# Second layer's output projection by seven quarter products

## The chip, the cores and the metric

The kernel runs on one core of one Trainium2 chip. A core has a matrix engine (PE, with its weight loads shown apart as PEld), VectorE (DVE), ScalarE (ACT), GpSimd (POOL), a queue engine that issues transfers (SP) and 16 DMA engines. The metric is device time in microseconds for one execution, the median of several runs. The profile is one execution taken by the hardware profiler.

## The reference

Two encoder layers over 512 tokens of width 1024. Layer 0 mixes tokens by neighbourhood attention (16 heads of 64, a window of 8 x 16 on a 64-wide grid), layer 1 by multi-head latent attention (16 heads). All is fp32.

```python
for i in range(DEPTH):                       # DEPTH = 2
    xn = rmsnorm(x, norm_g[i])
    y = mixer_na(...) if i % 2 == 0 else mixer_mla(...)
    h = x + y
    gate = jax.nn.sigmoid(rmsnorm(h, ple_norm[i]) @ ple_w_gate[i])   # 512x1024 @ 1024x1024
    x = h + gate * (p[i] @ ple_w_proj[i])
return rmsnorm(x, final_norm)
```

Both mixers end in `(o * silu(z)) @ w_out`: the heads' rows `o`, multiplied element by element by a gate branch, times a 1024x1024 matrix. That last product of layer 1 is what the change is about.

## The kernel before

**Precision.** Every fp32 matrix product is made of three passes in the format float32r: an operand is split into a rounded part `hi` (a copy on ACT) and a rest `lo` (a subtraction on POOL or DVE), and hi x hi, lo x hi and hi x lo are added up in PSUM. So a product of two 128x128 by 128x512 blocks is three matmuls, and every weight that comes from memory costs a copy of 128x1024 on ACT and a subtraction of the same size before PE can use it. `load_w` (L79 to L90) does that for one piece: a raw buffer (three in all), `whi`, `wlo` (three of each, in a pool shared by the whole kernel), or buffers `w4` of the stage's own pool.

**Stages.** Layer 0: the gate branch, the heads (`na_heads`), the output projection (`out_proj`), the embedding's gate (`gate_seven`). Layer 1: compressions (`mla_c`), the heads (`mla_heads`), `out_proj`, `gate_seven`, final norm.

**The latent attention** (`mla_heads`) is a loop of 70 steps. Step i takes scores of one query tile of one head (`score`: maximum on DVE L844, exponential on ACT L846, normalisation on POOL L848), transposes those of step i - 3 on PE (`turn`, L139), and every few steps multiplies by the values (`output`, L863). Projections of later heads and the product of the per-layer embedding (`ple`) are cut in pieces and laid among them. Two heads make one tile of rows; `gated` (L207 to L213) multiplies it by the gate branch `z` on POOL and splits it to `oT`, tile j of which holds rows 128 j to 128 j + 127 of `o` transposed.

**The output projection** (`out_proj`, L411 to L428) goes by halves n of the output's 1024 columns and by the four token tiles t. Each of the eight results is 24 matmuls of 128x512 into a bank of PSUM; DVE adds it to the residual row (L427), and `turn_h` (L1043) then scales the row on DVE (L1047), transposes it on PE and hands it to `keep_half` (L538), which makes the gate's operands from it. The residual rows `r` are loaded from memory at the start of the stage (L1035).

**The gate** (`gate_seven`, L568) already multiplies by Strassen's scheme in Winograd's form: tokens, inner dimension and output columns are each cut in two, and the eight quarter products become seven, with sums of quarters on both sides. The sums of the weights' quarters are made by DMA in memory: `sum_step` issues, on POOL's queue, a copy or an accumulating transfer of 1 MB; eight of these make a layer's four sums. The heads of layer 0 issue them for both layers, one per head (16). The sums of the activations are made in `keep_half` and `mixed`.

**Order.** On each engine instructions run in the order of the program that the build's planner settles, with its own estimates of durations. `tc.issue_after(x)` puts what follows behind x on that engine's queue. Buffers of a pool are taken from those that are free.

## Time and profile before

| what | value |
|---|---|
| time, median of 3 runs | 657.52 us (657.03 to 657.75) |
| span of the profiled execution | 655.8 us; the page gives no other time of it |
| PE busy | 646.2 us (99% of the span) |
| DVE, ACT, POOL busy | 398.1, 441.2, 433.8 us (61, 67, 66%) |
| DMA | 102.18 MB, mean 156 GB/s |
| heads of layer 1 | to about 565 us |
| output projection of layer 1 on PE | about 554 to 608 us, first matmuls among the last heads' |
| gate of layer 1 on PE | about 608 to 647 us |

PE's busy time counts matmuls whose ends are modelled, so that 99% says that PE always had a matmul under way, not that it ran at its peak. Rows of a view by stretch give the stretch, its length, then busy time and count for each engine, the granted clock of PE (1.00 is full), the share of DMA time and the rate. Rows of a view in order of time give start and length, both in us; "x3" is three of them, one behind the other; in square brackets stands the idle time before and what ended it. Rows of groups give busy time and the mean in ns of one.

### The profile page before, as it was taken

The numbers are of one execution on the slowest core, as the hardware profiler recorded it, in microseconds if no ns is written. First come the engines' busy times: TensorE is split into PE (matmuls) and PEld (weight loads), VectorE is DVE, ScalarE is ACT, GpSimd is POOL, SyncE is SP. The second block draws the span as 40 slices with busy tenths as digits, with TensorE's granted clock in tenths as the row PEclk, the third lists the DMA queues.
The fourth block names the chain that finished last, engine by engine and source line by source line (L and its number), as shares of the span: only waits on it lengthen the run. The fifth ranks groups of instructions, "written<-read, shape, count | busy, mean of one in ns | idle before, by whom it ended". The sixth has DMA issues, their size and how long they took to land.

```text
span 655.8 us, 10132 instructions
## 1 busy us (share of the span) xinstructions
PE 646.2 (99%) x3419; PEld 551.6 (84%) x3419; DVE 398.1 (61%) x854; ACT 441.2 (67%) x879; POOL 433.8 (66%) x383
## 2 busy tenths in 40 slices
PE   9999999999999999999999999999999999999994
PEld 6888888998988888888899888888888888888884
DVE  6190355845646526569825613888888886464665
ACT  7672587766767743687743635897979897537855
POOL 0496475895685664697764626785969887436974
PEclk9999999999999999999999999999999999999998
DMA  9944254996675889435743334120111223673524
GB/s 329 348 134 140 96 197 134 249 233 143 215 161 184 199 171 373 169 129 157 252 120 114 103 98 148 51 76 5 64 55 65 65 71 123 226 287 129 191 67 160
DMA packets 44756, 102.18 MB, mean 156 GB/s; under 512 B 4640, under 2 KB 17696, under 8 KB 44704
## 3 DMA queue, kind: packets, MB, share of 16 engines
q1 hardware_dynamic: 33776, 83.97, 38.1%
q0 software_dynamic: 10496, 16.78, 11.8%
q10 hardware_dynamic: 432, 0.79, 0.3%
q8 instruction: 27, 0.44, 0.3%
q14 instruction: 25, 0.20, 0.1%
HBM read 89.99 MB, written 25.17 MB: 176 GB/s over the span
## 4 chain that ended last, share of the span: by engine, by line
PE 98%; ACT 0%; DVE 0%; issue 0%; POOLq 0%; POOL 0%
PE ps_mm L107 35%; PE ps_S L107 12%; PE ps_mm L751 7%; PE ps_T L139 6%; PE ps_T L643 5%; PE ps_O L863 5%; PE ps_mm L643 3%; PE ps_S L643 3%; PE ps_T L107 3%; PE ps_T L238 2%; PE ps_O L400 2%; PE ps_O L107 2%; PE ps_mm L701 2%; PE ps_mm L184 2%; PE ps_T L388 2%; PE ps_S L701 1%
## 5 line engine op out<-in xcount | busy, mean ns | idle before, releaser
L84 POOL TENSOR_TENSOR wwlo<-wraw,wwhi 128x1024 fp32r<-128x1024 f32 (+5 forms) x78 | 143.2, 1852 | 76.4 <-ACT wwhi L83 54.7
L83 ACT ACTIVATE wwhi<-wraw 128x1024 fp32r<-128x1024 f32 (+5 forms) x81 | 65.5, 832 | 61.1 <-issue 19.2
L588 POOL TENSOR_TENSOR wlo<-wraw,whi 128x512 fp32r<-128x512 f32 x56 | 73.6, 1346 | 25.2 <-ACT whi L586 19.0
L848 POOL TENSOR_TENSOR ex<-ex,rc 128x512 f32<-128x512 f32 x64 | 66.3, 1045 | 25.8 <-DVE rc L847 22.0
L846 ACT ACTIVATE ex<-ps_S,mx 128x512 f32<-128x512 f32 x64 | 44.0, 688 | 11.7 <-DVE mx L844 10.1
L844 DVE TENSOR_REDUCE mx<-ps_S 128x1 f32<-128x512 f32 x64 | 43.7, 682 | 8.3 <-PE ps_S L107 7.7
L96 DVE TENSOR_TENSOR pt_lo<-ps_T,pt_hi 128x512 fp32r<-128x512 f32 x64 | 43.1, 681 | 7.1 <-ACT pt_hi L94 6.7
L374 POOL TENSOR_TENSOR ex<-ex,rc 128x128 f32<-128x128 f32 (+1 forms) x64 | 36.1, 621 | 15.0 <-DVE rc L370 15.0
L107 PE MATMUL ps_mm<-xh,wwhi 128*128 128x512 f32 x152 | 40.3, 398 | 0.0
L94 ACT ACTIVATE pt_hi<-ps_T 128x512 fp32r<-128x512 f32 x64 | 37.8, 595 | 3.4 <-PE ps_T L139 3.0
L107 PE MATMUL ps_mm<-xl,wwhi 128*128 128x512 f32 x152 | 38.5, 391 | 0.0
L139 PE MATMUL ps_T<-ident,ex 128*128 128x128 f32 x256 | 38.3, 272 | 0.0
L107 PE MATMUL ps_mm<-xh,wwlo 128*128 128x512 f32 x152 | 38.2, 391 | 0.0
L139 PEld LDWEIGHTS ps_T<-ident,ex 128*128 128x128 f32 x256 | 31.5, 140 | 7.5
L107 PEld LDWEIGHTS ps_mm<-xh,wwlo 128*128 128x128 f32 x152 | 28.3, 188 | 6.0
L586 ACT ACTIVATE whi<-wraw 128x1024 fp32r<-128x1024 f32 x28 | 29.2, 1055 | 5.9 <-DMA wraw<-sum 3.0
L107 PEld LDWEIGHTS ps_mm<-xl,wwhi 128*128 128x128 f32 x152 | 28.3, 188 | 5.7
L205 DVE TENSOR_TENSOR u<-ps_O,u 64x512 f32<-64x512 f32 x32 | 22.0, 686 | 17.2 <-ACT u L204 16.7
L368 ACT ACTIVATE ex<-ex,mx 128x128 f32<-128x128 f32 (+1 forms) x64 | 30.3, 475 | 2.7 <-DVE mx L358 1.8
L107 PEld LDWEIGHTS ps_mm<-xh,wwhi 128*128 128x128 f32 x152 | 27.3, 188 | 4.8
L209 POOL TENSOR_TENSOR u<-u,z 128x512 f32<-128x512 f32 x16 | 21.9, 1371 | 13.6 <-DVE u L205 8.3
L107 PE MATMUL ps_S<-ko,qo 128*128 128x512 f32 x96 | 28.9, 409 | 0.0
(441 smaller groups left out, 1849.8 us busy)
## 6 DMA issues: line engine op xcount, KB each, us to landing
sum<-gate POOLq DMA_DIRECT2D x12, 1024.0 KB, 7.8
wraw<-na_qk SPq DMA_DIRECT2D x16, 512.0 KB, 3.4
wraw<-sum SPq DMA_DIRECT2D x16, 512.0 KB, 3.3
pe<-pe SPq DMA_DIRECT2D x31, 256.0 KB, 6.9
wraw<-gate SPq DMA_DIRECT2D x12, 512.0 KB, 3.3
wraw<-na_v SPq DMA_DIRECT2D x8, 512.0 KB, 4.1
sum<-sum POOLq DMA_DIRECT2D x4, 1024.0 KB, 10.9
wraw<-na_o SPq DMA_DIRECT2D x8, 512.0 KB, 5.4
```

The lines of the kernel that those rows point to most:

```text
L83: nc.scalar.activation(hi[:, c], raw[:, c], AF.Copy)
L84: f = lambda e, c=c: e.tensor_tensor(out=lo[:, c], in0=raw[:, c], in1=hi[:, c].bitcast(F32), op=ALU.subtract)
L94: self.last_copy = nc.scalar.activation(hi, src, AF.Copy, scale=scale)
L96: nc.vector.tensor_tensor(out=lo, in0=src, in1=hi.bitcast(F32), op=ALU.subtract)
L107: last = self.last_mm = nc.tensor.matmul(out, l, r, start=i == 0, stop=i == n - 1)
L139: self.last_mm = self.nc.tensor.transpose(t[:, i * P:(i + 1) * P], b, self.ident)
L588: nc.gpsimd.tensor_tensor(out=lo[:, o], in0=raw[:, o], in1=hi[:, o].bitcast(F32), op=ALU.subtract)
L643: mm = nc.tensor.matmul(ps, l, r, start=j == 0 and p in banks, stop=j == 11 and p in (2, 3, 4), skip_group_check=True)
L751: self.last_mm = nc.tensor.matmul(PS[key], *terms[i], start=i == 0, stop=i == len(terms) - 1)
L844: nc.vector.reduce_max(mx, sp, axis=AX.X, negate=True)
L846: nc.scalar.activation(ex, sp, AF.Exp, bias=mx, accum_out=sm)
L848: nc.gpsimd.tensor_tensor(out=ex, in0=ex, in1=rc.to_broadcast([P, S]), op=ALU.mult)
```

## The change

The output projection of layer 1 is made by the same scheme of seven products (`out_seven`); layer 0 keeps `out_proj`. `MIXED` names the layers for which this holds.

- **Weights.** `sum_step` gets a key in place of a layer, and there is a third set of sums, for the matrix of the output projection. Layer 0's heads issue the sums of both gates, now those of layer 1 first. The eight transfers for the projection are issued in `score` of layer 1, one per head, behind the normalisation of the second query tile of heads 1 to 8.
- **Rows.** `gated_seven` takes the place of `gated` in layer 1. It writes the gated product over `z`, and mixes halves of tokens with DVE: for the first four tiles the difference goes to `oT` in place of the second half; for the other four, `zs` of tile j and of tile j - 4 are mixed in place.
- **Products.** `out_seven` loads 14 weight pieces (`piece_of`) in place of 8, splits the mixed rows to `Y` and `Y3`, and runs 7 x 2 x 12 matmuls, chained in one order. Products 2, 4, 5 and 3 go on in the bank in which 1, 7 and 6 ended, which DVE reads in between. What DVE reads is added to or taken from the residual rows, up to three rows per half product.
- **The gate's operands** come in another order of rows, so that `keep_mixed` makes them, the operand of product 3 among them (before: `mixed(3)`, in the gate).
- **Order of loads.** The residual rows are loaded behind the first four weight pieces. `gn`, and the gate's loads of the embedding, follow the last weight load of the projection, which is now its fourteenth.

```diff
+MIXED = (1,)
+LO, HI = slice(0, 256), slice(256, 512)
...
+        for key in [("gate", l) for l in SEVEN] + [("out", l) for l in MIXED]:
+            self.sums[key] = {p: dram.tile([2 * P, D], F32, name=f"sum{key[0]}{key[1]}{p}") for p in (4, 5, 6, 7)}
...
-            attend(j, lambda e: self.sum_step(l, 2 * step + e))
+            key = (("out", 0) if 0 in MIXED else ("gate", 1), ("gate", 0))[j // 4]
+            attend(j, lambda e: self.sum_step(key, 2 * (j % 4) + e))
...
+    def piece_of(self, pool, key, p, c, after=None, rest=None):
...
+        own = self.pieces % (3 + self.wxn // 2) < 3
+        self.pieces += 1
+        src = self.quarter[key][p] if p < 4 else self.sums[key][p]
+        raw = self.wp.tile([P, 1024], F32, name="wraw", tag="wraw", bufs=3)
+        q, n = (self.wp, 3) if own else (pool, self.wxn)
+        hi, lo = (q.tile([P, 1024], F32R, name=t, tag=t if own else "w4", bufs=n) for t in ("whi", "wlo"))
+        self.last_load = nc.sync.dma_start(raw, src[c * P:(c + 1) * P])
+        with self.tc.issue_after(after.ins) if after else nullcontext():
+            nc.scalar.activation(hi, raw, AF.Copy)
+        for o in (slice(0, S), slice(S, 2 * S)):
+            (rest or nc.gpsimd).tensor_tensor(out=lo[:, o], in0=raw[:, o], in1=hi[:, o].bitcast(F32), op=ALU.subtract)
...
+    def gated_seven(self, u, zs, oT, j):
...
+        nc.gpsimd.tensor_tensor(out=z, in0=u, in1=z, op=ALU.mult)
+        sub = lambda o, x, y: nc.vector.tensor_tensor(out=o, in0=x, in1=y, op=ALU.subtract)
...
+        if g == 0:
+            sub(u[:, HI], z[:, LO], z[:, HI])
+            for x, c in ((z, LO), (u, HI)):
+                nc.scalar.activation(hi[:, c], x[:, c], AF.Copy)
+                nc.gpsimd.tensor_tensor(out=lo[:, c], in0=x[:, c], in1=hi[:, c].bitcast(F32), op=ALU.subtract)
+            return
+        nc.scalar.activation(hi, z, AF.Copy)
+        nc.gpsimd.tensor_tensor(out=lo, in0=z, in1=hi.bitcast(F32), op=ALU.subtract)
+        y = zs[k]
+        sub(y[:, HI], y[:, HI], z[:, HI])
+        sub(y[:, LO], y[:, LO], y[:, HI])
+        sub(z[:, LO], z[:, LO], y[:, LO])
...
+    def out_seven(self, pool, layer, oT, zs, res, after, last_mm):
...
+        order = (1, 7, 2, 4, 6, 5, 3)
+        prep = lambda p: W.__setitem__(p, [self.piece_of(pool, key, p, c, rest=nc.vector if c and p in (1, 7, 2) else None)
+                                           for c in range(2)])
+        for p in order[:2]:
+            prep(p)
+        for t in range(NT):
+            nc.sync.dma_start(res[t], self.a["x"][t] if layer == 0 else self.spill[t])
+        for p in order[2:4]:
+            prep(p)
...
+        for k in range(4):
+            nc.scalar.activation(Y[0][:, k, :], zs[k], AF.Copy)
+            nc.vector.tensor_tensor(out=Y[1][:, k, :], in0=zs[k], in1=Y[0][:, k, :].bitcast(F32), op=ALU.subtract)
+        for k in range(4):
+            nc.scalar.activation(y3[0][:, k, :], zs[4 + k][:, LO], AF.Copy)
+            nc.vector.tensor_tensor(out=y3[1][:, k, :], in0=zs[4 + k][:, LO], in1=y3[0][:, k, :].bitcast(F32),
+                                    op=ALU.subtract)
+        src = {1: ([x[0] for x in oT], 0), 7: ([x[0] for x in oT], 256), 2: ([x[1] for x in oT], 0),
+               4: ([x[1] for x in oT], 256), 6: (Y, 0), 5: (Y, 256), 3: (y3, 0)}
+        banks = {1: "mm", 7: "S", 6: "T"}
+        home = {2: 1, 4: 7, 5: 6, 3: 6}
...
+        for n, p in enumerate(order):
+            if 0 < n < 4:
+                prep(order[n + 3])
...
+            for i in range(2):
...
+                for j, (l, r) in enumerate(m):
+                    with self.tc.issue_after(mm):
+                        self.last_out = nc.tensor.matmul(ps, l, r, start=j == 0 and p in banks,
+                                                         stop=j == 11 and p in (2, 4, 3), skip_group_check=True)
+                    mm = self.last_out.ins
+                for t, h, op in {1: ((0, 1, 0), (2, 1, 0), (2, 0, 1)), 7: ((2, 1, 0),), 2: ((0, 0, 1),), 4: ((2, 0, 1),),
+                                 6: ((2, 0, 0),), 5: ((2, 1, 1),), 3: ((0, 1, 1),)}[p]:
+                    r = res[t + i][:, h * S:(h + 1) * S]
...
+                if p in (2, 6, 5, 3):
+                    after(t + i, h)
...
+    def keep_mixed(self, t, n, ps):
...
+        if (t < 2, n) == (True, 0):
+            self.operand(1, i, ps)
+            keep = self.AC[i] = self.temp("a")
+            nc.scalar.activation(keep, ps, AF.Copy)
+        elif n == 0:
+            c = self.C[i] = self.temp("c")
+            nc.scalar.activation(c, ps, AF.Copy)
+            nc.vector.tensor_tensor(out=ps, in0=self.AC[i], in1=ps, op=ALU.subtract)
+            self.operand(7, i, ps)
+            nc.scalar.activation(self.AC[i], ps, AF.Copy)
+        elif t >= 2:
+            self.operand(4, i, ps)
+            nc.vector.tensor_tensor(out=self.C[i], in0=self.C[i], in1=ps, op=ALU.subtract)
+            nc.vector.tensor_tensor(out=ps, in0=self.AC[i], in1=ps, op=ALU.add)
+            self.operand(6, i, ps)
+            nc.scalar.activation(self.AC[i], ps, AF.Copy)
+        else:
+            self.last_pair = self.operand(2, i, ps)
+            nc.vector.tensor_tensor(out=ps, in0=ps, in1=self.AC[i], op=ALU.subtract)
+            self.operand(3, i, ps)
...
+            norm = nc.gpsimd.tensor_tensor(out=ex, in0=ex, in1=rc.to_broadcast([P, S]), op=ALU.mult)
+            step = h - 1
+            if qt == 1 and 0 <= step < 8 * len(later):
+                with self.tc.issue_after(norm.ins):
+                    self.sum_step(later[step // 8], step % 8)
...
-                    ps = self.transposes([hg[:, i * P:(i + 1) * P] for i in range(4)])
+                    ps = self.transposes([hg[:, i * P:(i + 1) * P] for i in range(4)],
+                                         "O" if layer in MIXED and t % 2 else "T")
...
+                if layer in MIXED:
+                    self.out_seven(pool, layer, oT, zs, res, turn_h, last)
```

107 lines of the change are left out of this document (61 added, 46 removed).

## Prediction

> **What bounds the kernel now.** I read the page first: the engines' busy time and the shares of the chain of waits.
>
> ```profile
> span 655.8 us, 10132 instructions
> PE 646.2 (99%) x3419; PEld 551.6 (84%) x3419; DVE 398.1 (61%) x854; ACT 441.2 (67%) x879; POOL 433.8 (66%) x383
> PE 98%; ACT 0%; DVE 0%; issue 0%; POOLq 0%; POOL 0%
> ```
>
> PE is the chain for 98% of the span. A matmul taken off PE is a saving, unless PE then waits. So I looked at the other engines around the place of the change, with busy time by stretch (columns: stretch, length, PE, PEld, DVE, ACT, POOL, granted clock, DMA share, GB/s).
>
> ```profile
> 400.00:492.00 92.00, 92.00 (x508) 77.90 (x508) 75.99 (x152) 77.13 (x170) 68.42 (x66) 1.00 0.20 58
> 464.00:480.00 16.00, 16.00 (x98) 13.84 (x97) 14.31 (x30) 14.41 (x33) 15.68 (x16) 1.00 0.29 79
> 554.00:570.00 16.00, 16.00 (x78) 13.25 (x77) 5.45 (x8) 8.51 (x14) 6.89 (x5) 1.00 0.44 150
> 570.00:586.00 16.00, 16.00 (x77) 13.32 (x77) 12.16 (x11) 4.77 (x6) 5.34 (x3) 1.00 0.94 360
> 586.00:608.00 22.00, 22.00 (x108) 18.30 (x107) 10.52 (x18) 16.45 (x27) 15.45 (x14) 1.00 0.36 121
> 608.00:641.00 33.00, 33.00 (x160) 27.82 (x159) 23.78 (x38) 22.19 (x38) 28.18 (x23) 1.00 0.39 128
> ```
>
> PE has no gap anywhere, at full clock. The attention of the second layer (first two rows) leaves POOL 15.68 of 16 us busy in its densest stretch. The output projection (554 to 608) has spare POOL and ACT time, but 0.94 of the DMA at 570 to 586. The gate behind it keeps POOL at 28.18 of 33 us.
>
> **Removed: 24 matmuls.** The projection has 2 x 4 x 24 = 192 matmuls of 128x512; seven products of 2 x 12 are 168. The chain of waits prices a steady stream of that shape in the gate, which already works by seven products.
>
> ```profile
> 625.08 16.32 PE ps_T L643 x72
> ```
>
> 16.32 / 72 = 0.2267 us, times 24 = **5.44 us saved**. The 32 transposes of `turn_h` stay, so PE gains no work. The bounds are 0 and 5.44: all the rest of the change can only make PE wait.
>
> **Added in the attention: eight accumulating DMAs on POOL.** The first layer's heads issue 16 such DMAs before and after, in another order. The eight new ones go one per head, behind the normalisation of its second query tile. Six read a quarter, two read a sum.
>
> ```profile
> L522 POOL DMA_DIRECT2D sum<-gate x12: 771/922/1347, 89.3 to 234.5; - x12
> L522 POOL DMA_DIRECT2D sum<-sum x4: 1274/1294/1313, 125.2 to 224.6; - x4
> sum<-sum POOLq DMA_DIRECT2D x4, 1024.0 KB, 10.9
> ```
>
> That is 6 x 0.922 + 2 x 1.294 = 8.1 us of POOL's time within the first stretch above, where POOL idles 92.00 - 68.42 = 23.6 us. Behind each issue wait the next normalisation, its transposes on PE, and what follows them. The last sum lands some 11 us after its issue, over 50 us ahead of the projection, so landing costs nothing. How late may a normalisation be? Here POOL's row of two of them, and PE's transposes of the first:
>
> ```profile
> 466.76 2.03 POOL L848 TENSOR_TENSOR ex<-ex,rc 128x512 f32<-128x512 f32 x2
> 468.46 0.60 PE L139 MATMUL ps_T<-ident,ex 128*128 128x128 f32 x4
> ```
>
> The first is done at 466.76 + 1.015 = 467.78, 0.68 us ahead of its transposes, in the densest of the stretches. One issue of 0.92 in the queue before it makes PE wait 0.25 us or so; the eight issues meet two or three such places. I take **+0.6 us**; the bounds are 0 and 8.1 (every issue on PE's path).
>
> **Added: the mixing of gated rows.** `gated_seven` adds DVE subtractions of 128x256: one for each of the first four head pairs, three for each of the others, 16 in all. By the 0.43 us row below, 6.9 us, of which DVE has 92.00 - 75.99 = 16.0 us free in the first 92 us alone. The splits of `Y` and `Y3` (four of 512 and four of 256 on ACT and on DVE) are needed by the fifth product, 96 matmuls or 21.8 us after the first begins, and at 0.69 us and less a piece they take some 4.5 us of each engine. Taken at 0, bounds 0 and 1.
>
> ```profile
> L649 DVE TENSOR_TENSOR ps_S<-ps_S,s 128x256 f32<-128x256 f32 x1 | 0.4, 424 | 0.0
> ```
>
> **Moved: which weights the first matmuls need.** This is where I expect the gain to leak. Before, all tokens start on the first weight piece; after, a product consumes two pieces in 5.44 us, and the matmuls are chained in one order. The end of attention, by the chain of waits and by the rows of the weight splits:
>
> ```profile
> 561.10 0.69 DVE L96 TENSOR_TENSOR pt_lo<-ps_T,pt_hi 128x512 fp32r<-128x512 f32 x1 [0.37 <-ACT pt_hi L94]
> 554.73 1.39 PE ps_S L107 x6
> 561.13 1.15 PE ps_S L107 x5
> 562.28 1.37 PE ps_mm L107 x6
> 563.65 1.81 PE ps_O L863 x8
> 544.96 1.06 ACT L83 ACTIVATE wwhi<-wraw 128x1024 fp32r<-128x1024 f32 x1 [0.50 <-PE ps_mm L751]
> 562.05 1.23 DVE L84 TENSOR_TENSOR wwlo<-wraw,wwhi 128x1024 fp32r<-128x1024 f32 x1 [0.26 <-ACT wwhi L83]
> 563.53 2.39 POOL L84 TENSOR_TENSOR wwlo<-wraw,wwhi 128x1024 fp32r<-128x1024 f32 x1 [7.40 <-ACT wwhi L83]
> 568.75 2.94 ACT L83 ACTIVATE ww<-wraw 128x1024 fp32r<-128x1024 f32 x3
> 569.83 1.47 DVE L84 TENSOR_TENSOR ww<-wraw,ww 128x1024 fp32r<-128x1024 f32 x1 [3.01 <-ACT ww L83]
> 570.83 2.73 POOL L84 TENSOR_TENSOR ww<-wraw,ww 128x1024 fp32r<-128x1024 f32 x1 [0.60 <-ACT ww L83]
> 578.82 2.39 POOL L84 TENSOR_TENSOR ww<-wraw,ww 128x1024 fp32r<-128x1024 f32 x1 [5.26 <-ACT ww L83]
> L1035 SPq DMA_DIRECT2D r<-spill x4: 383/423/443, 566.4 to 567.8; - x4
> DMA to landing us min/median/max: 2.8/4.1/6.7
> ```
>
> Before, some 17 projection matmuls stand among the last heads' work up to 563.65, all on the first piece. After, that piece serves six (first half of product 1, tokens 0 to 127); the next six need the second piece, whose buffers the per-layer embedding holds until 561 and whose rest is done at 562.05 + 1.23 = 563.3. So 11 matmuls (2.5 us) lose their place as cover. The last output products can move up to fill most of it, since their last operand is there at 561.10 + 0.69 = 561.8: I leave 0.7 us open. From 563.3 PE has 18 matmuls of product 1 and six of product 7 (third piece, ready at 565.9) = 5.4 us, to 568.7. The fourth piece, on the `w4` buffers, came at 569.83 + 1.47 = 571.3; the heads' last rows are let go one split earlier now (`u` is read only by the product with `z`), so about 570: 1.0 us more. Product 2 accumulates into the bank of product 1, and waits until DVE has read it three times per half, for all four residual rows. The last of these landed at 567.8 + 6.7 = 574.5, about when product 7 ends (570 + 18 x 0.2267 = 574.1): 0.2 us. Product 4 wants its pieces at 580; they follow the raw buffers, behind the residual rows, to about 580 and 582.5. The norm and embedding loads, tied behind the last weight load, now leave that stretch and help. Together **+1.9 us**; the bounds are 0 (all overlap) and 5.4 (three full halves and the bank wait in a row).
>
> **Added: work behind each product.** DVE adds 18 products' reads to rows in place of 8; more than that, the products 6, 5 and 3 share one pair of banks, so that each half waits until DVE has read the half before it, with 12 matmuls = 2.72 us of other work in between. By rows of 0.69 (one read), 0.75 (`hg`) and 0.69 (operands), DVE has 2.8, 4.2 and 3.5 us behind each half of these three: 21.0 in all, against 3 x 5.44 + 24 x 0.109 (a transpose) = 18.9 of PE.
>
> ```profile
> L427 DVE TENSOR_TENSOR r<-ps_mm,r 128x512 f32<-128x512 f32 x4 | 2.8, 692 | 4.5 <-PE ps_mm L107 4.5
> 583.13 0.75 DVE L1047 SCALAR_TENSOR_TENSOR hg<-r,rowb,gp 128x512 f32<-128x512 f32 x1
> 604.04 0.87 PE ps_T L139 x8
> ```
>
> The 2.1 us of lag fall mostly on the gate's first two products (10.9 us of cover, their operands come from products 2 and 6). I take **+0.4**, bounds 0 and 2.1. Without the cover it is 2.1.
>
> **Added: six more pieces to split.** ACT is busy 51.9 of the 87 us from 554 to 641 (the last four stretches), and six pieces at 1.05 add 6.3. POOL gets 11 projection pieces (three of 14 go to DVE) where it had four. Its rate, in the gate, below the last rows that the heads leave it, and PE's last matmul:
>
> ```profile
> 568.93 1.29 POOL L213 TENSOR_TENSOR o1l<-u,o1h 128x512 fp32r<-128x512 f32 x1 [0.74 <-ACT o1h L212]
> 604.30 10.50 POOL L588 TENSOR_TENSOR wlo<-wraw,whi 128x512 fp32r<-128x512 f32 x8
> 615.28 7.56 POOL L588 TENSOR_TENSOR wlo<-wraw,whi 128x512 fp32r<-128x512 f32 x6
> 624.13 3.33 POOL L588 TENSOR_TENSOR wlo<-wraw,whi 128x512 fp32r<-128x512 f32 x2 [1.28 <-issue]
> 646.59 0.40 PE L643 MATMUL ps_O<-wlo,X 128*128 128x256 f32 x2
> ```
>
> 10.50 / 4 = 2.63 us a piece, against 2.72 us that PE takes to use one: POOL just keeps up, so 0, with the case that it doesn't as a rival.
>
> **The sum.** 655.8 - 5.44 + 0.6 + 1.9 + 0.4 = 653.3 for the profiled span. The median of the runs, 657.52, is 1.7 above that span (the page gives no other time of that execution), so **655.0 us**.
>
> **Rivals.** *Full gain*: the planner, which settles each engine's order, closes all holes: 657.52 - 5.44 = 652.1. For it: PE has no gap before, with all these waits around. Against: the first pieces' times. *Gain used up*: the start costs 5 in place of 1.9, or several terms come near their upper ends: 657.4. For it: a product wants two pieces every 5.44 us from a standing start, on a DMA at 0.94. *POOL becomes the bound* (slower): from 568.9, where the last heads' rows are on POOL, 23 pieces remain to it until the end, with four small powers and one product (3.5 us), and 18 matmuls (4.1 us) run after the last piece. The last matmul of before ends at 646.9, so the point from which it decides is (646.9 - 568.9 - 3.5 - 4.1) / 23 = 3.06 us a piece. Two rows stand below it (2.63, 2.52), one above (3.33). At 3.2 the end moves by 23 x 0.14 = 3.2 us: 660.7. What could lift it is DVE work beside it:
>
> ```profile
> 579.26 3.17 DVE L1047 SCALAR_TENSOR_TENSOR hg<-r,rowb,gp 128x512 f32<-128x512 f32 x2
> 571.73 2.92 DVE L84 TENSOR_TENSOR ww<-wraw,ww 128x1024 fp32r<-128x1024 f32 x1 [0.42 <-ACT ww L83]
> ```
>
> Both ran while POOL split weights; alone the two would have taken 1.5 and 1.22. The Trainium skill, "SBUF — State Buffer", section "SBUF: two separate sides", says that DVE operations with two SBUF inputs and GpSimd operations take a shared port pair in turn, and the loser waits for the whole instruction. These two rows agree. By that rule each of the added `Y` rests would stand between two of POOL's, an estimate of 4 x 0.69 + 4 x 0.43 = 4.5 us over 23 pieces, or 2.83 a piece: near the point, not over it; the sum stays at 655.0 by the rule and by the rows, and the rule is why this rival has more than a token chance. *The DMA issues push the attention* (slower): all 8.1 us on PE's path, with the other terms, 655.0 - 0.6 + 8.1 = 662.5; half of it, 658.5. Against: 23.6 us of idle POOL.
>
> **Chances.** Forecast 0.40, its own range 653.0 to 656.2; full gain 0.20; gain used up 0.18; POOL the bound 0.15; attention pushed 0.07. A measurement can tell 0.2% (1.3 us): faster 0.60, same 0.18, slower 0.22. The range is 651.8 to 659.6: below lies nothing that PE's count allows but the spread of runs, above about the half of the two slow cases.
>
> **What would show it.** 168 matmuls of 128x512 in place of 192. PE gaps between 554 and 583, ended by weight splits or by DVE's reads: 1 to 3 us in all; none says full gain, over 4 says used up. Gaps before L139's transposes between 418 and 490: under 1 us. In the gate, PE waiting for POOL's rests would show the POOL rival; a piece then takes over 3 us. I am wrong as well if the last matmul ends under 2 us or over 5 us earlier than 646.9.

## The result, and the profile after

The changed kernel takes **681.31 us** (median; 679.05 to 683.75), against 657.49 for the kernel before beside it: ratio 1.0364, 95% interval 1.0340 to 1.0389. The forecast was 655.0, its range ended at 659.6. The first lines of the page, and the shares of the chain of waits:

```profile
span 677.3 us, 10188 instructions
...
PE 649.9 (96%) x3395; PEld 551.6 (81%) x3395; DVE 424.4 (63%) x890; ACT 451.8 (67%) x897; POOL 465.3 (69%) x413
...
PE 79%; DVE 7%; ACT 5%; POOL 4%; DMA 3%; issue 2%; POOLq 0%; SPq 0%; DVEq 0%; ACTq 0%
```

The 24 matmuls are gone (3419 to 3395), but PE's busy time rose by 3.7 us, and PE is the chain for 79% of the span in place of 98%. The same stretches as before, and two more (columns as before: stretch, length, PE, PEld, DVE, ACT, POOL, granted clock, DMA share, GB/s):

```profile
400.00:492.00 92.00, 88.25 (x468) 74.13 (x467) 77.11 (x142) 71.67 (x159) 73.08 (x74) 0.96 0.51 131
464.00:480.00 16.00, 12.25 (x48) 9.47 (x48) 13.92 (x22) 8.88 (x21) 11.21 (x12) 0.79 0.47 128
469.00:478.00 9.00, 7.71 (x26) 6.06 (x27) 7.24 (x16) 5.91 (x15) 6.10 (x6) 0.62 0.31 118
...
570.00:586.00 16.00, 12.97 (x48) 9.55 (x46) 13.25 (x19) 6.58 (x12) 9.09 (x6) 0.89 0.86 311
586.00:608.00 22.00, 20.12 (x93) 16.41 (x94) 12.76 (x19) 11.18 (x14) 20.04 (x15) 1.00 0.66 212
608.00:641.00 33.00, 24.30 (x120) 20.46 (x119) 22.25 (x34) 26.77 (x41) 30.81 (x26) 0.85 0.58 189
```

At 464 to 480 PE did 48 matmuls where it did 98, with POOL busy for 11.21 us and not fuller than before (15.68). And the clock, 1.00 in every stretch before, is 0.62 to 0.89 where PE had stood still. PE's own rows show the stops (in square brackets the idle time and what ended it):

```profile
468.98 0.63 PE L147 MATMUL ps_T<-ident,ex 128*128 128x128 f32 x4 [2.46 <-POOL o1l L554]
470.90 1.65 PE L115 MATMUL ps_S<-ke,qe 96*128 96x512 f32 x3 [1.29 <-ACT ex L951]
...
578.13 0.73 PE L605 MATMUL ps_S<-whi,o1h 128*128 128x512 f32 x2 [1.48 <-ACT whi L537]
586.27 0.70 PE L605 MATMUL ps_mm<-whi,o1h 128*128 128x512 f32 x2 [1.72 <-DVE r L612]
602.70 0.66 PE L147 MATMUL ps_T<-ident,hg 128*128 128x128 f32 x4 [1.61 <-DVE hg L1158]
...
631.07 1.12 PE L147 MATMUL ps_O<-ident,hg 128*128 128x128 f32 x4 [2.57 <-ACT a L675]
638.31 1.19 PE L748 MATMUL ps_O<-whi,X 128*128 128x256 f32 x4 [6.13 <-DVE X L628]
```

These seven are 17.3 us; smaller ones make it 18.0. The ledger: the span grew by 677.3 - 655.8 = 21.5 us although 5.44 were saved, so the change cost 26.9. Of that 18.0 are gaps of PE; the other **8.9 us, the remainder, are matmuls that ran slower behind the gaps**. By stage the gaps are 4.4 us in the attention, 4.8 in the projection and 8.7 in the gate; from the spacing of the same matmuls before and after I count another 3.6, 2.7 and 2.4 us for the clock.

### The profile page after: what moved, and what is told of

The parts are those of the page before. It is cut to its first block, busy times and chain, and to the rows that moved or that the text cites. A ratio compares the mean times of both kernels' runs of the same rounds, so it can differ in the third digit from the quotient of the medians.

```text
span 677.3 us, 10188 instructions
## 1 busy us (share of the span) xinstructions
PE 649.9 (96%) x3395; PEld 551.6 (81%) x3395; DVE 424.4 (63%) x890; ACT 451.8 (67%) x897; POOL 465.3 (69%) x413
## 3 DMA queue, kind: packets, MB, share of 16 engines
q0 software_dynamic: 15744, 25.17, 17.3%
## 4 chain that ended last, share of the span: by engine, by line
PE 79%; DVE 7%; ACT 5%; POOL 4%; DMA 3%; issue 2%; POOLq 0%; SPq 0%; DVEq 0%; ACTq 0%
PE ps_mm L115 30%; PE ps_S L115 8%; PE ps_T L748 5%; PE ps_mm L856 4%; PE ps_T L147 4%; PE ps_mm L748 2%; PE ps_T L246 2%; PE ps_O L972 2%; PE ps_O L407 2%; PE ps_S L748 2%; PE ps_mm L806 2%; PE ps_T L115 2%; PE ps_mm L192 2%; PE ps_T L395 2%; POOL wlo L539 1%
## 5 line engine op out<-in xcount | busy, mean ns | idle before, releaser
L92 POOL TENSOR_TENSOR wwlo<-wraw,wwhi 128x1024 fp32r<-128x1024 f32 (+5 forms) x76 | 139.1, 1852 | 67.0 <-ACT wwhi L91 45.4
L539 POOL TENSOR_TENSOR wlo<-wraw,whi 128x512 fp32r<-128x512 f32 x78 | 105.2, 1380 | 30.3 <-ACT whi L537 25.6
L91 ACT ACTIVATE wwhi<-wraw 128x1024 fp32r<-128x1024 f32 (+5 forms) x78 | 62.5, 824 | 60.1 <-issue 19.1
L953 POOL TENSOR_TENSOR ex<-ex,rc 128x512 f32<-128x512 f32 x64 | 68.8, 1095 | 24.3 <-DVE rc L952 17.5
L537 ACT ACTIVATE whi<-wraw 128x1024 fp32r<-128x1024 f32 x42 | 44.1, 1057 | 20.2 <-DMA wraw<-sumout 7.8
L115 PE MATMUL ps_S<-ke,qe 96*128 96x512 f32 x96 | 29.4, 415 | 1.3 <-ACT ex L951 1.3
```

The lines of the kernel that those rows point to most:

```text
L91: nc.scalar.activation(hi[:, c], raw[:, c], AF.Copy)
L92: f = lambda e, c=c: e.tensor_tensor(out=lo[:, c], in0=raw[:, c], in1=hi[:, c].bitcast(F32), op=ALU.subtract)
L115: last = self.last_mm = nc.tensor.matmul(out, l, r, start=i == 0, stop=i == n - 1)
L537: nc.scalar.activation(hi, raw, AF.Copy)
L539: (rest or nc.gpsimd).tensor_tensor(out=lo[:, o], in0=raw[:, o], in1=hi[:, o].bitcast(F32), op=ALU.subtract)
L953: norm = nc.gpsimd.tensor_tensor(out=ex, in0=ex, in1=rc.to_broadcast([P, S]), op=ALU.mult)
```

## The experiments: the gate and its one bank

**Reading.** The kernel's PSUM banks go by the names mm, S, T and O; there are 2, 2, 3 and 1 of them. Before, transposes of finished rows went to the three T banks. Now those of odd rows go to bank O, of which there is one, and which the gate also uses for the last half of its product 7 (a half of 256 columns). These are the rows of ACT and DVE around the gap at 638, with POOL's weight rests beside them:

```profile
630.42 0.60 ACT L675 ACTIVATE a<-ps_O 128x512 f32<-128x512 f32 x1 [0.27 <-DVE X L628]
...
632.36 0.58 ACT L627 ACTIVATE X<-ps_O 128x512 fp32r<-128x512 f32 x1
```

```profile
632.97 0.69 DVE L628 TENSOR_TENSOR X<-ps_O,X 128x512 fp32r<-128x512 f32 x1 [2.25 <-ACT X L627]
633.58 0.69 DVE L678 TENSOR_TENSOR ps_O<-ps_O,a 128x512 f32<-128x512 f32 x1
634.18 3.39 DVE L628 TENSOR_TENSOR X<-c,X 128x512 fp32r<-128x512 f32 x2
637.49 0.68 DVE L628 TENSOR_TENSOR X<-ps_O,X 128x512 fp32r<-128x512 f32 x1
```

```profile
625.42 20.75 POOL L539 TENSOR_TENSOR wlo<-wraw,whi 128x512 fp32r<-128x512 f32 x16
```

Row 3 holds the bank until ACT's copy `a` at 630.4 (first gap, 2.57 us), then row 1's second half goes in and is read five times, the last read behind two operands of product 5 (`X<-c,X`) that take 1.7 us each. Only then may product 7 start its last half: 6.13 us. Two runs take the bank away from one or the other user.

*a_bankT*: one of the four odd transposes to T.

```diff
-                                         "O" if layer in MIXED and t % 2 else "T")
+                                         "O" if layer in MIXED and t % 2 and (t, n) != (1, 1) else "T")
```

> The changed kernel with one bank moved: the last transposes of the projection (row 1, second half) go to a bank of the three T in place of the single O, which the gate's product 7 needs for its last half. Theory (the O bank is the wait in the gate): both PE gaps between 628 and 638 us of the changed kernel, 2.57 and 6.13 us, shrink to under 1 us together, and with them the stretch at reduced clock behind them, so 671 to 673 us. Rival (the operands are late because DVE and POOL are behind, and the bank only shows it): PE then waits as long for the operands of product 2 or 6, and the time stays within 2 us of 681.

Measured 676.67, ratio 1.0291 (1.0276 to 1.0307): 4.6 us won, about half of what was expected, since row 3 still held the bank, now in front of the same matmul:

```profile
634.67 1.22 PE L748 MATMUL ps_O<-whi,X 128*128 128x256 f32 x4 [4.41 <-ACT a L675]
```

*e_gatebank*: the gate leaves O.

```diff
-                        C[p, i, o] = self.psum("O" if o else banks[p])[:, :wd]
+                        C[p, i, o] = self.psum("T" if o else banks[p])[:, :wd]
...
-                        q = self.psum("mm" if i else "T")
+                        q = self.psum("mm" if i or layer else "T")
```

> The changed kernel with the split half of the gate's product 7 of layer 1 in a bank of the three T, and both difference banks of product 5 in mm, so that nothing in the gate uses the O bank that the odd rows' transposes use. Moving the last transposes alone gave 4.7 us of the 8 to 10 expected and left a wait of 4.41 us on the O bank for row 3's copy. Theory (the one O bank is the whole wait): no PE gap over 1.5 us between 620 and 650, 671 to 673 us. Rival (the operands behind are late anyway, the half only moves): a gap of 3 us or more ahead of product 2 or 6, 675 or more.

Measured 675.33 (672.17 to 677.00), ratio 1.0268 (1.0238 to 1.0298): 6.0 us won, less than the 8 to 10 expected, and a time just within the rival's 675 or more. But both gaps go; one of 2.09 is left, ended by an operand and shorter than the rival's 3 us:

```profile
636.13 1.31 PE L748 MATMUL ps_mm<-whi,X 128*128 128x512 f32 x3 [2.09 <-ACT X L627]
```

So both waits were for the bank, and the bank cost about 6 us; the rest of the wait was for the operand. The same edit on another version of the kernel (*g_both* below, against f) won 4.7.

## The experiments: issues and mixing in the attention

Four runs divide the two parts that the change adds there.

*c_nosums*: the eight transfers are not issued, and plain quarters stand in for the sums.

```diff
-                with self.tc.issue_after(norm.ins):
-                    self.sum_step(later[step // 8], step % 8)
+                pass
...
-        src = self.quarter[key][p] if p < 4 else self.sums[key][p]
+        src = self.quarter[key][p] if p < 4 else self.quarter[key][p % 3 + 1] if key[0] == "out" else self.sums[key][p]
```

> The changed kernel without the eight summing DMAs in the attention; the four products on summed weights read plain quarters in their place, so the projection is computed from other weights, with the same loads and the same instructions behind them. Theory (the mixing on DVE makes the wait in the attention, the issues add little): the gap at 469 us stays, the time falls by at most 2 us. Rival (the issues fill POOL and delay the normalisations): the gaps of the attention vanish and the time falls by 6 to 9 us.

*d_before_sums*: the kernel before, with the eight transfers issued at the same places (their sums are used by nothing).

```diff
...
+            norm = nc.gpsimd.tensor_tensor(out=ex, in0=ex, in1=rc.to_broadcast([P, S]), op=ALU.mult)
+            if qt == 1 and 1 <= h <= 8:
...
+                with self.tc.issue_after(norm.ins):
+                    self.sum_step(2, h - 1)
```

> The kernel before, with the eight summing DMAs alone added in the attention at the places of the change, into memory that nothing reads. The prediction priced them at 0.6 us: 657.5 to 658.7. The rival priced half of their 8.1 us or more on PE's path: 661 or more.

*b_subpool*: all mixing subtractions on POOL.

```diff
-        sub = lambda o, x, y: nc.vector.tensor_tensor(out=o, in0=x, in1=y, op=ALU.subtract)
+        sub = lambda o, x, y: nc.gpsimd.tensor_tensor(out=o, in0=x, in1=y, op=ALU.subtract)
```

> The changed kernel with the 16 subtractions that mix the gated rows on POOL in place of DVE. Theory (a DVE instruction that reads two SBUF operands cannot begin while POOL runs without a break, and one of these stood 6.02 us and held the scores' maxima behind it): the 2.46 and 1.29 us gaps at 469 to 471 us and the slow clock behind them go, POOL gains about 11 us of work, and the time falls by 4 to 8 us, to 673 to 677. Rival (POOL is simply too full in the attention, by the eight DMA issues): 11 us more of POOL work makes it worse, 683 or more.

*f_sums_early*: the transfers issued ahead of the attention, among the gate branch's projections.

```diff
+            if also:
+                with self.tc.issue_after(self.last_rest.ins):
+                    also(j)
...
+        also = lambda j: self.sum_step(later[0], j)
+        zs.update(self.z_phase(a["mla_z"], xT, range(NEARLY), also=also))
...
```

> The changed kernel with the eight summing DMAs issued in the gate branch of layer 1 ahead of the attention, one behind each weight split on POOL, where POOL idles over half of the time. Theory (mixing alone and issues alone cost about 1 us each, only both together fill POOL so far that a DVE instruction with two SBUF operands waits 6 us): the attention ends as without the sums, 672 to 674 us. Rival (the issues cost the same wherever POOL works, or the queue blocks on a sum that has not landed): 678 or more.

| run | time, us | ratio to before (95%) | gaps of PE in the attention |
|---|---|---|---|
| issues and mixing (the change) | 681.31 | 1.0364 (1.0340 to 1.0389) | 2.46 and 1.29 at 469 to 471 |
| mixing without issues (c) | 672.59 | 1.0233 (1.0214 to 1.0251) | none over 0.4 |
| issues without mixing (d) | 658.18 | 1.0012 (1.0003 to 1.0022) | 0.38 |
| mixing on POOL (b) | 684.76 | 1.0403 (1.0361 to 1.0444) | 0.52 at 469, 6.00 at 486 |
| issues earlier (f) | 686.70 | 1.0450 (1.0432 to 1.0467) | 2.44 at 371 (ahead of the attention), 4.78 and 0.58 at 414 to 416 |

Beside the mixing the issues cost 681.31 - 672.59 = 8.7 us; without it they cost 0.7, the prediction's term. So c came out by its rival's numbers (the gaps go, 6 to 9 us are won) and d by the prediction's: neither "the mixing" nor "the issues" is the cause by itself. What the mixing costs without the issues no run gives as a time; c has no gap over 0.4 us in the attention.

b and f came out as slow as their rivals said, 683 and 678 or more, but by another wait. In both the two gaps at 469 to 471 are down to 0.52 us or gone. In b PE then waited 6.00 us for the rotated queries:

```profile
485.69 0.80 PE L115 MATMUL ps_S<-ke,qe 96*128 96x512 f32 x1 [6.00 <-DMA qe<-rl]
```

POOL had made them by 478.98; it was their transfer of 64 KB that landed late, at 485.64, 6.63 us behind its issue, where the same one took 1.94 in the kernel before. A summing transfer of 1 MB had been issued 2.7 us ahead of it, at 476.33. In f the summing transfers, of 7 to 13 us each, were under way beside the loads ahead of the first scores: the load of the rotation's table was issued at 403.24, where the changed kernel issued it at 392.65, and the first queries came late behind it. So the issues have a second way to make PE wait, through the transfers beside them, and b and f do not decide between POOL's load and the mixing. b also waited 10.37 us at bank O.

What meets? These are POOL's and DVE's rows of the changed kernel ahead of the gap at 469. POOL first:

```profile
458.35 1.31 POOL L524 DMA_DIRECT2D sumout<-sumout  x1
459.16 1.81 POOL L546 TENSOR_TENSOR z<-u,z 128x512 f32<-128x512 f32 x1
460.42 2.54 POOL L953 TENSOR_TENSOR ex<-ex,rc 128x512 f32<-128x512 f32 x2
462.41 3.02 POOL L92 TENSOR_TENSOR wwlo<-wraw,wwhi 128x512 fp32r<-128x512 f32 x2
464.90 1.77 POOL L892 TENSOR_TENSOR rl<-rl,rope_s 128x512 f32<-128x512 f32 x1
466.15 1.20 POOL L554 TENSOR_TENSOR o1l<-z,o1h 128x256 fp32r<-128x256 f32 x1
468.17 0.73 POOL L554 TENSOR_TENSOR o1l<-u,o1h 128x256 fp32r<-128x256 f32 x1 [0.82 <-ACT o1h L553]
```

DVE and ACT:

```profile
460.97 0.76 DVE L890 STREAM_SHUFFLE rl<-rh 128x512 f32<-128x512 f32 x1
461.62 6.02 DVE L547 TENSOR_TENSOR u<-z 128x256 f32<-128x256 f32 x1
467.56 0.68 DVE L891 TENSOR_TENSOR rh<-ps_mm,rope_c 128x512 f32<-128x512 f32 x1
468.16 1.27 DVE L104 TENSOR_TENSOR pt_lo<-ps_T,pt_hi 128x512 fp32r<-128x512 f32 x2
467.67 0.42 ACT L553 ACTIVATE o1h<-u 128x256 fp32r<-128x256 f32 x1 [4.33 <-DVE u L547]
```

The mixing subtraction, 0.43 us in the forecast, took **6.02 us**. It began in a run of POOL work and ended at 467.64, just behind POOL's first idle moment (466.15 + 1.20 = 467.35). Behind it on DVE stood the rope product, two rests of turned scores (`pt_lo`) and a maximum; behind that, PE. (PE's row at 468.98 names POOL's `o1l`, but that one stood behind the same subtraction, by way of ACT's copy, which waited 4.33 us for it.) The shuffle just before it, with one input, took its normal time beside the same POOL work. Without the issue (c) the same subtraction at the same place took 0.97, although POOL was busy back to back there too:

```profile
459.62 2.23 POOL L953 TENSOR_TENSOR ex<-ex,rc 128x512 f32<-128x512 f32 x2
461.82 2.55 POOL L92 TENSOR_TENSOR wwlo<-wraw,wwhi 128x512 fp32r<-128x512 f32 x2
```

```profile
459.98 0.97 DVE L547 TENSOR_TENSOR u<-z 128x256 f32<-128x256 f32 x1
```

The difference is in POOL's records (start plus length is the end of one). In c they overlap by 0.03 to 0.05 us (459.62 + 2.23 = 461.85, the next starts at 461.82). Behind this issue, which took 1.31 us, each starts 0.50 to 0.55 us ahead of the end of the one before (460.42 + 2.54 = 462.96, the next at 462.41). There DVE's subtraction found no place through five POOL instructions. The records overlap like this behind four of the eight issues, those of 1.28 to 1.36 us, and not behind the others, of 0.77 to 0.90.

Of the four subtractions of the first group this was the only long one. The first (441.25, 1.26 us) also began in such an overlapping run, but one that ended soon: it was done 0.3 us behind POOL's first idle moment, as the long one was. The other two took 0.74 and 0.97.

The Trainium skill, "SBUF — State Buffer", section "SBUF: two separate sides", has it that DVE operations with two SBUF inputs and GpSimd operations hold a shared port pair in turn, each for a whole instruction. The kind of operation agrees with these rows (two inputs held up, one input not); the length does not: it was a run of five POOL instructions, not one.

Two runs test that. *i_oneinput* changes the four operations and nothing else on any engine's queue; it leaves the subtraction out, so the second halves of these rows are not mixed and the output is another:

```diff
-            sub(u[:, HI], z[:, LO], z[:, HI])
+            nc.vector.stream_shuffle(u[:, HI], z[:, HI], list(range(32)))
```

> The changed kernel, with the mixing subtraction of each of the first four head pairs (two inputs in SBUF, 128x256, four in all) replaced by a shuffle of the same size on the same engine at the same place in its order, which reads one input; the subtraction is left out, so the second half of these rows is not mixed. Nothing else on any engine moves. Theory 1 (that DVE subtraction is held up as long as POOL has work back to back, and the 6.02 us one is what starts the gaps at 469 and 471): the four shuffles take under 0.9 us each, no gap of PE over 0.5 us is left between 450 and 500, the last output matmul of the attention comes 7 to 8 us earlier than 571.7, the time is 673 to 675. Rival (POOL is simply full there with issues, products and rests, whatever DVE does): gaps of 1.5 us or more stay near 469, the time is 679 to 682.

*m_sums_moved* (on top of e_gatebank) moves the issues to other steps of the loop, and keeps the subtraction:

```diff
-            step = h - 1
-            if qt == 1 and 0 <= step < 8 * len(later):
+            at = (5, 9, 13, 16, 18, 28, 30, 33)
+            if i in at:
...
-                    self.sum_step(later[step // 8], step % 8)
+                    self.sum_step(later[0], at.index(i))
```

> The kernel with the gate's halves out of bank O, and the eight summing transfers issued at other places of the attention: none of them between about 453 and 475, where POOL is fullest, four of them ahead of it one step earlier or later than before, four behind it. Theory 1 (only the issues in that stretch make the difference, they make POOL's run back to back that holds DVE's subtraction): no gap of PE over 0.5 us between 450 and 500, 667 to 670. Theory 2 (issues and mixing cost wherever they meet on POOL and DVE): a gap of 1 us or more at another place of the attention, 672 to 678.

i took **672.97** us, ratio 1.0246 (1.0217 to 1.0275); m took **669.94**, ratio 1.0195 (1.0137 to 1.0253). That median hides a split: two of its four runs took 666.18 and 667.02 us, two 672.85 and 674.49. The profile is of the one at 667.02; what the long two met is not on record. The four operations by groups (busy time, mean ns of one) and the stretch 464 to 480, of i:

```profile
L551 DVE STREAM_SHUFFLE u<-z 128x256 f32<-128x256 f32 x4 | 1.8, 445 | 0.0
```

```profile
464.00:480.00 16.00, 15.49 (x93) 13.11 (x93) 13.70 (x28) 13.47 (x31) 16.00 (x18) 1.00 0.54 148
```

and of m:

```profile
L547 DVE TENSOR_TENSOR u<-z 128x256 f32<-128x256 f32 x4 | 5.0, 1244 | 0.0
```

```profile
464.00:480.00 16.00, 15.59 (x93) 13.20 (x92) 14.16 (x30) 13.66 (x32) 15.86 (x17) 1.00 0.43 141
```

In i POOL is busy 16.00 of 16 us, as full as it can be, with all its issues in place, and PE loses half a microsecond. So it is not POOL's load that stops PE; it is the DVE operation held up by it, and in these runs only where an issue stands ahead of a run of POOL work. Theory 1 holds in i, and in the execution of m that was profiled; m's long runs leave room for its second theory.

## The experiments: do the parts add up

*g_both* is e with f, *h_both_ypool* also puts the rests of `Y` and `Y3` on POOL, *k_bank_oneinput* is e with i.

> The two edits of the runs before it in one: early sums, and the gate's half off the O bank. If the two waits are separate, their gains add: 663 to 665 us. If the gate's operands are the limit, about 668.

```diff
-            nc.vector.tensor_tensor(out=Y[1][:, k, :], in0=zs[k], in1=Y[0][:, k, :].bitcast(F32), op=ALU.subtract)
+            nc.gpsimd.tensor_tensor(out=Y[1][:, k, :], in0=zs[k], in1=Y[0][:, k, :].bitcast(F32), op=ALU.subtract)
...
```

> As the run with early sums and the moved half, and the rests of Y and Y3 on POOL in place of DVE. Theory (DVE instructions with two SBUF operands and POOL's splits hold each other up at the start of the projection: the three rests of Y3 took 2.68 us in place of 1.2 and held the last heads' rows): 1 to 3 us less than without, 660 to 663. Rival (POOL is the scarce one from there on): 1 to 4 us more.

> The one-input shuffle in place of the four mixing subtractions (which are left out) and the gate's halves kept out of bank O, together. If both causes are what they seem and lie in stages behind one another, they add up: 681.3 - 6.0 (bank alone) - 6.5 to 8 (shuffle alone) = 667 to 669, with no gap of PE over 0.5 us left in the attention and under 2.5 us in the gate; what is left above 652 is then the projection's start. Rival: as with the sums moved ahead, a wait elsewhere takes the place of the one removed, 671 or more.

g 681.96 (ratio 1.0374, 1.0324 to 1.0424) and h 684.33 (1.0408, 1.0377 to 1.0438), where 663 to 665 and 660 to 663 were expected: both carry f's late queries (4.50 and 5.47 us at 413 to 414), so they say nothing of `Y`. k took **668.49** (1.0159, 1.0138 to 1.0179), where 681.3 - 6.0 - 8.3 = 667.0 would be the exact sum: the two causes stand in different stages and nearly add up. k is 16 us above 652.1; 9.5 of its 10.8 us of gaps lie in the projection and the gate.

## The experiments: the projection's start, and what came behind it

In m, where the attention and bank O are clear, product 2 waits 3.33 us for its bank (a bank mm, in which product 1 ended). PE's row, DVE's rows ahead of it, and the loads of the residual rows `r` with their times from issue to landing:

```profile
579.55 0.70 PE L605 MATMUL ps_mm<-whi,o1h 128*128 128x512 f32 x2 [3.33 <-DVE r L612]
```

```profile
573.18 1.78 DVE L582 TENSOR_TENSOR Yl<-z,Yh 128x512 fp32r<-128x512 f32 x1
574.98 0.69 DVE L614 TENSOR_TENSOR r<-r,ps_mm 128x512 f32<-128x512 f32 x1
575.59 1.68 DVE L539 TENSOR_TENSOR wlo<-wraw,whi 128x512 fp32r<-128x512 f32 x2
577.19 0.41 DVE L585 TENSOR_TENSOR Y<-z,Y 128x256 fp32r<-128x256 f32 x1
577.53 1.27 DVE L614 TENSOR_TENSOR r<-r,ps_mm 128x512 f32<-128x512 f32 x2
578.72 0.68 DVE L612 TENSOR_TENSOR r<-ps_mm,r 128x512 f32<-128x512 f32 x1
```

```profile
L574 SPq DMA_DIRECT2D r<-spill x4: 382/430/451, 567.9 to 569.3; - x4
DMA to landing us min/median/max: 6.1/7.3/8.5
```

DVE has no idle time there: rests of `Y` and of a weight stand between the adds. But the rows are late as well: the four landed at 574.05, 575.31, 576.60 and 577.87, and two of the three adds that free the bank need the third. (In *n_copy1* below DVE itself waited 0.18 us for the first of them.) Product 7 was done at 576.22. An estimate from these rows: with nothing else on DVE the two adds would have ended 1.3 us behind the landing, at 577.9 in place of 579.40, so about 1.5 of the 3.33 us are DVE's queue and 1.8 the row's landing.

The clock hides part of this wait in the changed kernel. There the matmuls of product 7 ran slowly behind the gap of 1.48 and product 2 waited only 1.72 us; in m they ran at full clock and it waited 3.33. From the end of the gap of 1.48 to product 2 it is 8.14 us in the one and 8.16 in the other, so the slow clock cost nothing there by itself.

Six runs worked on the projection and the gate behind it.

*j_rows_first* (on k): the residual rows ahead of the first weights on SP's queue.

```diff
+        for t in range(NT):
+            first = nc.sync.dma_start(res[t], self.a["x"][t] if layer == 0 else self.spill[t])
+        with self.tc.issue_after(first.ins):
+            [prep(p) for p in order[:2]]
-        for t in range(NT):
-            nc.sync.dma_start(res[t], self.a["x"][t] if layer == 0 else self.spill[t])
```

> As the run with shuffle and bank together, but the residual rows are loaded ahead of the first two pairs of weight pieces in place of between the second and third pair; the order of PE differs a little with it (the last output matmuls of the attention ahead of the projection's first). Against that run: theory 1 (product 2 waits for DVE's adds because the rows land late): PE's gap ahead of product 2 (1.7 us in the changed kernel, at 586) falls under 0.5 us, the slow stretch of the clock behind 578 is shorter, 2 to 4 us less time. Theory 2 (DVE has too much queued there: rests of weights, mixing, adds): the gap stays over 1 us and the time within 1 us. Third: the first weights come later by the rows' 6 us of transfer, and the gap moves to product 1 or 7: 1 to 4 us more.

677.66 (1.0310, 1.0294 to 1.0325), 9 us worse than k: the third case by its mechanism, at more than twice its 1 to 4 us. The first weight piece landed at 573.86 in place of k's 567.22, and PE stood 10.56 us ahead of the projection's first matmul:

```profile
574.99 1.22 PE L605 MATMUL ps_mm<-whi,o1h 128*128 128x512 f32 x2 [10.56 <-ACT whi L537]
```

So the rows cannot go first. With them landed by 572.58 PE had no gap ahead of product 2, but this run doesn't show that they alone were the wait, since its late start gave DVE time as well.

*n_copy1* (on m): product 1's halves copied by ACT, the adds read the copy. *o_defer* (on m): `after(t, h)` behind both halves of a product. *p_copy_defer*: both.

```diff
+                    if p == 1 and (t, h, op) == (0, 1, 0):
+                        one = pool.tile([P, S], F32, name="one", tag="one", bufs=2)
+                        nc.scalar.activation(one, ps, AF.Copy)
+                    if p == 1:
+                        ps = one
```

```diff
-                    after(t + i, h)
+                    held.append((t + i, h))
+                if i:
+                    with self.tc.issue_after(mm):
+                        for x in held:
+                            after(*x)
+                    held = []
```

> The kernel with moved sums and the gate out of bank O, and product 1's two half results copied once by ACT to SBUF; DVE's three adds of each to residual rows read the copy, so that the bank is free for product 2 after one copy of 0.6 us. Left in the kernel it starts from: a gap of 3.33 us ahead of product 2, ended by DVE's add, and 2.4 us in which the matmuls behind it run at a lower clock. Theory (product 2 waits for its bank behind a full DVE queue): both go, the last matmul of the projection comes 4.5 to 6 us earlier than 614.6, the time falls by as much: 664 to 665.5. Rival (the weights of product 2, whose rests stand in the same DVE queue and on POOL, are next to come late): a gap of 1.5 us or more stays there, ended by a weight's rest or its copy, and 2 us or less are won.

> The kernel with moved sums and the gate out of bank O, where the scaling and transposes of a finished row come behind the second half of the product that finishes it, in place of between its halves. Left in the kernel it starts from: a gap of 2.12 us at 598, where the transposes of the row that product 6 finishes stand on PE right behind its last matmul and wait for DVE's add (0.69) and scaling (1.30), with 1.7 us at a lower clock behind it. Theory: the gap goes, 3 to 4 us less, 666 to 667. Rival (the gate's first operands then come later, and the wait moves to the gate): the gap at the start of the gate grows from 0.83 to 2 us or more, and the time stays within 1.5 us.

> Both of these together. If they add up, 660 to 662.5: the projection then has one gap of 1.5 us left (ACT's copy of the fourth weight piece, whose buffer comes free with the last heads' rows). Rival: one wait takes the other's place, 664 or more. In no case below 656: seven products do not pay here unless the stalls at the start of the projection go as well.

n 668.35 (1.0170, 1.0155 to 1.0185), where 664 to 665.5 was expected: the gap at 579 goes, so the bank was the wait, and a new one stands at 587:

```profile
586.81 0.74 PE L147 MATMUL ps_T<-ident,hg 128*128 128x128 f32 x4 [4.18 <-DVE hg L1163]
```

The adds now have two inputs in SBUF, take up to 1.76 us each beside POOL's splits in place of 0.68, and DVE is as late as it was. o **666.95** (1.0143, 1.0126 to 1.0161), within the 666 to 667 expected: its gap of 2.12 at 598 goes and the projection's last matmul comes 4.6 us earlier (609.9 for 614.6). But the gate gave all of it back (2.08 us for its operand `X`, and a clock of 0.83 at 620 to 640): the profiled executions of m and o span 665.2 and 665.6 us, so between these two executions its rival held, and the 3 us between the medians are m's two long runs.

p 668.82 (1.0179, 1.0147 to 1.0211): the rival held. n's gap stays (4.09 us at 586), and PE now waits in the gate for POOL's weight rests, four times; the longest of them:

```profile
651.56 0.50 PE L758 MATMUL ps_S<-wlo,X 128*128 128x512 f32 x1 [1.04 <-POOL wlo L539]
```

The four are 2.6 us, and POOL is busy 20.00 of 20 us at 620 to 640. *r_both_dve* and *q_defer_dve* move four of the gate's weight rests to DVE, on p and on o.

```diff
-            W[p] = [self.piece_of(pool, ("gate", layer), p, c, after) for c in range(2)]
+            W[p] = [self.piece_of(pool, ("gate", layer), p, c, after, nc.vector if layer and c and p in (6, 5, 3, 4) else None) for c in range(2)]
```

> The kernel with product 1's copies and the deferred rows together, and of the gate's last four products (6, 5, 3, 4) the second weight piece's rest on DVE in place of POOL: four of 22 pieces behind 580 us, some 10 us of POOL's work. Left in the kernel it starts from: POOL busy 20.0 of 20 us at 620 to 640, and 2.6 us of PE's gaps in the gate ended by POOL's rests (L539). Theory (with the earlier waits gone POOL's splits set the gate's pace): these gaps go, the last matmul of the gate comes 3 to 5 us earlier than 657.4, 664 to 666. Rival (DVE, slowed by POOL in its two-input operations, is late with operands in its turn): gaps ended by DVE's X or wlo take their place, 667 or more.

> The kernel with the deferred rows alone, and the same four rests of the gate on DVE. Left there: no gap ended by POOL, but 0.6 and 2.1 us at 626 and 629 ended by ACT (a and X, read from bank O and from the transposed row), and a clock of 0.83 at 620 to 640. Theory (what bounds that gate is the chain through bank O: transposes, ACT, DVE, transposes, one bank): the gap at 629 stays and the time stays within 1.5 us of 667. Rival (POOL is what holds it): 664 or less.

r 666.90 (1.0141, 1.0126 to 1.0156): POOL's gaps fall to 0.72 us and 1.9 us are won, with DVE's own wait of 1.40 at 643 in their place; that lies between its two cases. PE's last matmul ends 3.2 us earlier than in p, but the final norm behind it gives half of that back. q 667.10 (1.0147, 1.0130 to 1.0164): nothing won, as expected where PE does not wait for POOL. No version came below the kernel before; the best stand at 666.9, and none behind m has a profiled span more than 0.2 us under m's 665.2.

## Why the prediction was wrong, by its own steps

- **24 matmuls, 5.44 us.** Right: 168 for 192.
- **The eight issues, +0.6 us (bounds 0 and 8.1).** Their own price was right (d: 0.7; six at 0.85 and two at 1.30 us, rows below), but not beside the mixing. I priced two additions of one stage one by one; beside the mixing the issues cost 8.7 us (c).
- **The mixing, 0 (bounds 0 and 1).** This step failed. The row I priced it by (L649, 0.43 us) reads one input from PSUM; the mixing reads two from SBUF. Its four subtractions of the first group took 2.25 us on average, one 6.02, and that one stopped PE; by i the four cost 8.3 us where the issues are. And "DVE has 16.0 us free" is a sum over 92 us; what counted was who stands behind the operation in DVE's queue. I did weigh that DVE and POOL hold each other up, but asked only how it slows POOL.
- **Moved weights and rows, +1.9 us (bounds 0 and 5.4).** Mechanism right, size not: in the changed kernel gaps of 1.48 (fourth piece, foreseen as 1.0), 1.72 (product 2's bank, foreseen as 0.2; 3.33 in m) and 1.61 (transposes right behind product 6, not foreseen), 4.8 us in all and up to 2.7 for the clock. For the bank I let the wait end with the landing of the rows and gave the adds behind it no time; the rows landed 1.7 us behind the end of product 7 in m (577.87 and 576.22) where I had 0.4, and by the estimate above DVE's other work is about as much again.
- **Work behind each product, +0.4 us (bounds 0 and 2.1).** Failed, and the step was the cover: "10.9 us" of the gate's first two products. The last half of the second needs bank O, which the new transposes hold. It cost 6.0 us by e, with 8.7 us of gaps in that stage. The line that names the bank was in the diff.
- **Six more pieces to split, 0.** Right for this kernel: POOL does one in 2.59 us (20.75 / 8, its row in the section on the bank) and PE waits for it nowhere in the gate. The rival of POOL as the bound, priced at 660.7, appeared in p only, at 2.6 us.

```profile
L524 POOL DMA_DIRECT2D sumout<-mla_o x6: 771/846/1357, 420.4 to 492.6; - x6
L524 POOL DMA_DIRECT2D sumout<-sumout x2: 1299/1304/1308, 458.4 to 484.5; - x2
```

- **A lower clock behind a gap** had no term: 8.9 us by the ledger, a third of the loss, of which 3.33 - 1.72 = 1.6 stood in place of a wait.
- **What would show it.** "Under 1 us" before the transposes at 418 to 490 was a good test (2.46 measured), and so was the end of the last matmul: 668.7, where an end less than 2 us ahead of 646.9 was to say that I am wrong. The test of the projection's start was weaker: the gaps ended by weight splits and DVE's reads are 1.48 + 1.72 = 3.2 us, just above the foreseen 1 to 3 and under the 4 of "used up".

**Open.** Of the 14.8 us that the best order that still computes the layer (o) keeps above 652.1, 9.1 are gaps: 3.3 for product 2's bank, 2.1 for the gate's operand, 1.5 for the fourth weight piece's buffer, the rest 0.6 or less each. I take the other 6 for the clock; no run held the clock and kept the gaps. Why POOL's records overlap by 0.50 to 0.55 us behind four of the eight issues, and not behind the others, wasn't tried.

## What to carry to other kernels

Where one engine is busy for 98% of the span, price an edit by the longest time that each added instruction can take at its place, and by what is queued behind it, not by free time summed over a stage. Two additions to one stage need a price together: here one was DMA issues on POOL, the other DVE operations with two SBUF inputs beside POOL's work, and neither alone shows the cost. And before a stage is called cover, list the PSUM banks that both stages use and how many of each there are.

## What the hardware showed that I had not expected

- A DVE subtraction of 128x256 with both inputs in SBUF took 6.02 us beside POOL work behind an accumulating DMA's issue, 0.97 beside the same work without that issue; a shuffle of that size with one input took 0.45 on average in the first surroundings (i).
- A transfer of 64 KB that landed in 1.94 us in the kernel before took 6.63 when it was issued 2.7 us behind a summing transfer of 1 MB (b), and PE stood 6.00 us for it.
- Gaps of PE of 2.46 and 1.29 us were followed by a granted clock of 0.62 for 9 us; in m, one of 2.12 was enough to slow the matmuls behind it (0.52 at 598 to 600). One of 1.48 slowed them in the changed kernel (0.73 at 580 to 586) and not in m (1.00 at 571 to 576). The Trainium skill, "TensorE: Matmul & The Clock Gate", section "HAM oscillation — how this bites in real kernels", warns of idle gaps over about 3.4 us; here shorter ones did it.
- With 18.0 us of gaps, PE's busy time rose by 3.7 us with 24 matmuls fewer: the page's 96% hides the slow clock.
